# Intermediate stores issued by GpSimd, S5 turns on ScalarE, later direct kernels and an undivided last product in a hybrid S5 and attention block

## The chip, the cores and the metric

The kernel runs on one core of one Trainium2 chip. The metric is device time in microseconds (us) of one launch. The profile comes from one further execution of the same program, recorded by the hardware profiler. The engines are TensorE (PE, matmuls; its weight loads are listed as PEld), VectorE (DVE), ScalarE (ACT), GpSimd (POOL) and SyncE (SP, which here only issues DMAs). Each engine works through its own queue in order; an instruction that waits holds what stands behind it.

## The reference

One layer over 512 tokens of width 2048, in f32:

```python
h = rmsnorm(x, norm_pre[l])
proj = h @ w_in[l]
u_s, g_s, q_d, k_d, v_d, g_d, q_x, g_x = jnp.split(proj, split_at, axis=-1)
y_s = jax.nn.gelu(s5_scan(u_s, ...))               # 64 groups x 16 channels, 64 complex states each
y_s = y_s * jax.nn.sigmoid(y_s @ w_glu[l] + b_glu[l]) * jax.nn.silu(g_s)
y_d = diff_attention(q, k, v, lam, lambda_init, diff_subln[l]) * jax.nn.silu(g_d)   # causal, 4 heads
mem_n = rmsnorm(mem, norm_mem[l])
y_x = memory_attention(q_x, mem_n, w_mem_kv[l]) * jax.nn.silu(g_x)                  # 256 memory tokens
mix = jnp.concatenate([y_s, y_d, y_x], axis=-1) @ w_out[l]
x = x + rmsnorm(mix, norm_post[l])
```

The S5 scan is a linear recurrence with a complex diagonal decay per state, driven through a matrix B, read out through a matrix C, plus a direct term.

## The kernel before, in words

**Weights.** All large matmuls split each f32 operand into a high and a low half and run three passes, high x high, low x high and high x low. A weight chunk is 128 x 1024 f32 (512 KB). SyncE loads it into one of two `raw` buffers, ScalarE casts the high half `whi`, VectorE subtracts to get the low half `wlo` (three buffers each), and TensorE uses both. The matmuls are issued by the helper at line 96, transposes at line 99, and all VectorE, ScalarE and SyncE work by one helper at line 71, so the profile tells instructions apart by their tiles.

**Order.** The list `chunks` holds all weight chunks in order. The main loop goes through it, and each chunk has four units of matmuls. Beside that, `at_slot(n, f)` puts side work into the dictionary `side` behind unit 4n + 3 (n in chunks, fractions being units). A scheduler turns this into the order on each engine; TensorE keeps the program's order of matmuls.

**Stages.** S0 makes the S5 input u, then the memory keys and values (16 chunks of `w_kv`), and prepares the S5 matrices. S5 follows with the gate and query projections (`w_in`) as its chunks and the scan as side work. S1 is the glu of the S5 branch, S2 the rest of `w_in` with the memory attention, S3 the differential attention, S4 the output projection, in which blocks of `w_out` are summed by DMAs from GpSimd (`sum_steps`), and a tail of last products and residual rows.

**S5.** The 64 groups are worked on in eight octets. In S0 each octet gets `s5_products` (line 540: VectorE forms `bp` and, in two halves of the generator, `dp`), `s5_maps` (line 566: four transposes of `bp` and a copy `up`) and `s5_weights` (line 573: small matmuls of `bp` with `dp`, the direct kernels, evacuated to `kz`). `dp`, `up` and `kz` go to DRAM (`sp_dr`, `k_dr`) and come back as `sp` and `tm` when the octet is scanned. In the scan `s5_angles` (line 632) turns the states' angles into cosine and sine in `cs`: the turns `iota` x `ftn`, a reduction by two VectorE instructions, and three activations on ScalarE, ahead of which a table is loaded. `s5_spread` (line 646) copies `up` into four blocks `ub`; `s5_states` (line 652) multiplies them with the input `us` on TensorE, then turns the result with `cs` (tiles `ra`), scans it (`zre`, `zim`) and turns it back into `x`; `s5_outputs` (line 689) multiplies `x` and `tm` out, applies the gelu and stores y in `y_dr`.

**Stores.** Results that a later stage reads again go through DRAM: the u columns, `dp`, `up` and `kz`, the memory keys and values `mk` and `mv`, the projections `ev` (gs, qx and gx), the gated S5 branch `tg` (to `ys_dr`), and the first two column blocks of the output projection (`omx`, to `mix_dr`). All of these are issued by SyncE, in one queue with the loads.

**Tail.** `last_product(i, c0, w)` (line 1267) makes w columns of the last block for token tile i, `c12_evac` and `residual` (line 1247) finish the rows and store them.

Of the kernel before, what the change touches and what calls it, by code (L numbers as in the profile page):

```python
# [19 lines left out]
P = 128  # L20
# [18 lines left out]
LCH = 4  # L39
# [15 lines left out]
def tile_hybrid_block(ctx: ExitStack, tc: tile.TileContext, a: dict, out: bass.AP):  # L55
# [134 lines left out]
    k_dr = [t_.rearrange("p (x e) -> (p x) e", x=4) for t_ in dram("k_dr", 4 * (2 * LCH - 1) * 16, 4)]  # L190
    gs_dr, qx_dr, gx_dr, ys_dr = dram("gs_dr", SEQ, 8), dram("qx_dr", SEQ, 4), dram("gx_dr", SEQ, 4), dram("ys_dr", SEQ, 8)

    chunks, side = [], {}

    def at_slot(n, f):
        side.setdefault(round(4 * n) + 3, []).append(f)
# [84 lines left out]
    def evac_mk():  # L281
        for h in range(4):
            mk = mp.tile([P, NMEM], F32, tag="mk", name="mk", bufs=2)
            v.tensor_tensor(mk, mkacc[h][:, :NMEM], rmb, ALU.mult)
            sy.dma_start(mk_dr[:, h * NMEM:(h + 1) * NMEM], mk)

    def evac_mv(b_, acc):
        mv = mp.tile([P, 512], F32, tag="mv", name="mv", bufs=1)
        s.activation(mv, acc, AF.Copy, scale=rm[:, b_:b_ + 1])
        sy.dma_start(mv_dr[:, b_ * 512:(b_ + 1) * 512], mv)  # L290


    h_raw = {}
# [19 lines left out]
    def evac_u(j, acc):  # L313
        ut = evp["p"].tile([P, LCH, NCH], F32, tag="ev", name="ut", bufs=2)
        v.tensor_tensor(ut, acc.rearrange("p (c s) -> p s c", s=LCH), rbp, ALU.mult)
        sy.dma_start(u_dr[j // 2][(j % 2) * P:(j % 2 + 1) * P], ut.rearrange("p s c -> p (s c)"))

    uacc = {}
    for c in range(NK // 2):
# [35 lines left out]
    def evac_to(dst):  # L355
        def f(i, acc):
            e_ = evp["p"].tile([P, SEQ], F32, tag="ev", name="ev", bufs=2)
            v.tensor_tensor(e_, acc, rb, ALU.mult)
            sy.dma_start(dst, e_)
        return f  # L360

    for j in range(8):
# [177 lines left out]
    def s5_products(o):  # L540


        bc = pt("bc", [512], 2)
        sy.dma_start(bc, a["bc"][o])
        gr = slice(8 * o, 8 * o + 8)

        def powers(t_, n):
            return t_[:, gr, :].unsqueeze(3).to_broadcast([P, 8, n, 16])

        def params(i, n):  # L550
            return bc[:, i * P:(i + 1) * P].rearrange("p (g h) -> p g h", g=8).unsqueeze(2).to_broadcast([P, 8, n, 16])

        bp, dp = pre["bp", o], pre["dp", o] = pt("bp", [8, LCH, 16]), pt("dp", [8, LCH + 1, 16], 2)
        m2 = pt("pm", [8, LCH + 1, 16])
        v.tensor_tensor(bp, powers(w1, LCH), params(0, LCH), ALU.mult)
        v.tensor_tensor(m2[:, :, 0:LCH], powers(w2, LCH), params(1, LCH), ALU.mult)
        v.tensor_tensor(bp, bp, m2[:, :, 0:LCH], ALU.add)
        v.tensor_tensor(dp, powers(pwr, LCH + 1), params(2, LCH + 1), ALU.mult)
        yield
        m2 = pt("pm", [8, LCH + 1, 16])  # L560
        v.tensor_tensor(m2, powers(npwi, LCH + 1), params(3, LCH + 1), ALU.mult)
        v.tensor_tensor(dp, dp, m2, ALU.add)
        sy.dma_start(sp_dr[o][:, 0:640], dp.rearrange("p g j h -> p (g j h)"))
        yield

    def s5_maps(o):
        pp_, up = psum("t"), pt("up", [512])
        for q in range(4):
            transpose(pp_[:, q * P:(q + 1) * P], pre["bp", o][:, 2 * q:2 * q + 2].rearrange("p x b h -> p (x b h)"))
        s.copy(up, pp_)  # L570
        sy.dma_start(sp_dr[o][:, 640:1152], up)

    def s5_weights(o):

        bp, dp, kz = pre["bp", o], pre["dp", o], pre["kz"][o % 2]
        kp = psum("t")
        for x in range(2):
            for q in range(4):
                mm(kp[32 * q:32 * q + 32, x * 64:(x + 1) * 64], bp[:, 2 * q + x, 0:2].rearrange("p b h -> p (b h)"),
                   dp[:, 2 * q + x, 0:LCH].rearrange("p j h -> p (j h)"), start=True, stop=True, tile_position=(0, 32 * q))  # L580
        s.copy(kz[:, :, LCH:], kp[:, 0:P].rearrange("p (x j h) -> p x j h", x=2, h=16)[:, :, 1:])
        for x in range(2):
            v.scalar_tensor_tensor(kz[:, x, LCH - 1], mask16, dsk[:, 2 * o + x:2 * o + x + 1],
                                   kp[:, x * 64:x * 64 + 16], ALU.mult, ALU.add)
        sy.dma_start(k_dr[o // 2].rearrange("(x o p) e -> o p x e", x=2, o=2)[o % 2], kz.rearrange("p x j h -> p x (j h)"))


    def s5_open():
# [43 lines left out]
    def s5_angles(o):  # L632

        cs = t512("cs", 2, (P, 2, 4, P))
        an, kr = cs[:, 0], cs[:, 1]
        g.tensor_tensor(an, iota.unsqueeze(1).to_broadcast([P, 4, P]),
                        ftn[:, 4 * o:4 * o + 4].unsqueeze(2).to_broadcast([P, 4, P]), ALU.mult)
        v.tensor_scalar(kr, an, MAGIC, None, ALU.add)
        v.scalar_tensor_tensor(an, kr, -MAGIC, an, ALU.add, ALU.subtract)
        c_, s_ = (cs[:, i].rearrange("p q c -> p (q c)") for i in range(2))  # L640
        s.activation(s_, c_, AF.Sin, scale=TURN)
        s.activation(c_, c_, AF.Abs)
        s.activation(c_, c_, AF.Sin, scale=-TURN, bias=halfpi)
        oct_[o]["cs"] = (c_, s_)
# [44 lines left out]
    def s5_outputs(o):  # L689

        d, us = s5["d"][o % 2], oct_[o]["us"]
        yp = psum("t")
        cols_ = [slice(q * P, (q + 1) * P) for q in range(4)]
        for q in range(4):
            mm(yp[:, cols_[q]], s5["d"][o // 2 % 2]["tm"][:, 4 * (o % 2) + q], us[:, q], start=q == 0, stop=False,
               skip_group_check=True)
        for q in range(4):
            for x in range(2):
                mm(yp[64 * x:64 * x + 64, cols_[q]], oct_[o]["dp"][:, 2 * q + x, 1:].rearrange("p j h -> p (j h)"),
                   d["x"][:, 2 * q + x, 0:NCH], start=False, stop=True, tile_position=(0, 64 * x), skip_group_check=True)  # L700
        if o % 2 == 0:
            s5["y"] = t512("ysb", 2, (P, 2, 512))
        ysb = s5["y"]
        sq = t512("sq")
        s.activation(sq, yp, AF.Square)
        v.scalar_tensor_tensor(sq, sq, 1.0 / GELU_A, yp, ALU.add, ALU.mult)
        s.activation(sq, sq, AF.Tanh, scale=GELU_A * GELU_S)
        v.scalar_tensor_tensor(ysb[:, o % 2], sq, 1.0, yp, ALU.add, ALU.mult)
        if o % 2 == 1:
            dst = y_dr[o // 2].rearrange("(q x h) (j c) -> j x h q c", x=2, h=16, j=LCH)  # L710
            for x in range(2):
                for j in range(LCH):
# [8 lines left out]
    for o in range(8):  # L721
        e = 9.5 + 1.75 * o if o < 4 else 17.5 + 3.25 * (o - 4)
        d = 2 if o < 4 else 4
        at_slot(e, lambda o=o: (oct_[o].setdefault("pr", s5_products(o)), next(oct_[o]["pr"])))
        at_slot(e + d / 2, lambda o=o: next(oct_[o]["pr"]))
        at_slot(e + 0.75 * d, lambda o=o: s5_maps(o))
        at_slot(e + (2 if o < 4 else 3), lambda o=o: s5_weights(o))
    at_slot(SG - 1, lambda: (s5_open(), s5_load(0), s5_u(0, 0), s5_u(0, 1), s5_load(1)))
    for x in range(2):
        at_slot(SG + 0.5 + x, lambda x=x: s5_toeplitz(0, x))  # L730
# [37 lines left out]
    def evac_glu(j, acc):  # L768
# [9 lines left out]
        v.scalar_tensor_tensor(tg, tg, 1.0, gt, ALU.add, ALU.mult)  # L778
        tgv, tzv = tg.rearrange("p (c t) -> p c t", t=LCH), tz.rearrange("p (t c) -> p c t", t=LCH)
        v.scalar_tensor_tensor(tgv, tzv, 0.125, tgv, ALU.mult, ALU.mult)  # L780
        sy.dma_start(ys_dr[j], tg)

    at_slot(S5_END, ge_open)
    at_slot(S1 + 1.5, rotary_tables)
# [445 lines left out]
    for n, (_, f) in enumerate(chunks):  # L1230
# [155 lines left out]
```

## Time and profile before

| | us |
|---|---|
| median of 3 timed runs | 816.15 (813.62 to 816.22) |
| profiled execution | 812.06 |
| its span | 810.0 |
| TensorE busy | 784.9 (97%) |
| VectorE busy | 590.4 (73%) |
| ScalarE busy | 381.7 (47%) |
| GpSimd busy | 76.5 (9%) |

The granted clock of TensorE is 0.992 on average. The DMA queue that SyncE fills moves 141.39 MB, that of GpSimd 16.78 MB. In the rows of a timeline the first two numbers are the start and the duration in us; a bracket gives the idle time of that engine before the row and what ended it. In the lists of waits the three numbers are the total time, the count and the longest wait. "SPq" and "POOLq" are the DMA-issuing instructions of SyncE and GpSimd.

### The profile page before, as it was taken

Reading aid. Unit: us, or ns where it says so; the run is one execution under the profiler, and the core shown is the slowest. Engines: PE = TensorE matmul, PEld = TensorE weight load, DVE = VectorE, ACT = ScalarE, POOL = GpSimd, SP = SyncE. Lnnn points to the kernel's source line nnn. Section 1 sums busy time; section 2 is a strip of 40 time slices with the busy share of each in tenths; the row PEclk is TensorE's granted clock in tenths of the full one; section 3 lists DMA queues with packets and bytes.
Section 4 is the critical chain, followed back from the end, with each engine's and each line's share of the span. In section 5 each row is a group of like instructions: output and inputs, shape, how many; then the busy total and the mean of one; then the engine's idle time right before and its main releaser. Section 6 shows DMA issues by size and latency. Waiting matters only on the chain.

```text
span 810.0 us, 11040 instructions
## 1 busy us (share of the span) xinstructions
PE 784.9 (97%) x3958; PEld 652.3 (81%) x3958; DVE 590.4 (73%) x1084; ACT 381.7 (47%) x619; POOL 76.5 (9%) x106
## 2 busy tenths in 40 slices
PE   8999999899999999999999999999999999999994
PEld 6877788788878888888877888888888787888884
DVE  4599877748998899846884554657988956774576
ACT  5654433434445445334723543356676643344451
POOL 0000000110000000002111221312201010000001
PEclk9999999999999999999999999999999999999998
DMA  7977767773655565358896854655623515349766
GB/s 250 355 265 259 256 199 248 257 227 89 185 159 158 139 171 160 117 153 299 259 255 239 234 169 144 156 182 159 157 77 103 156 55 205 131 138 330 288 210 254
DMA packets 66486, 158.87 MB, mean 196 GB/s; under 512 B 13568, under 2 KB 27008, under 8 KB 64768
## 3 DMA queue, kind: packets, MB, share of 16 engines
q1 hardware_dynamic: 63616, 141.39, 53.7%
q0 software_dynamic: 2816, 16.78, 8.6%
q8 instruction: 31, 0.51, 0.2%
q14 instruction: 23, 0.19, 0.1%
HBM read 134.68 MB, written 40.24 MB: 216 GB/s over the span
## 4 chain that ended last, share of the span: by engine, by line
PE 73%; DVE 11%; DMA 9%; ACT 3%; issue 2%; SPq 1%; POOL 1%; POOLq 0%; DVEq 0%; ACTq 0%
PE ps_mm L96 60%; PE ps_s L96 6%; PE ps_t L96 6%; DVE wlo L71 3%; DMA raw<-in_w_in_a_dram 2%; ACT whi L71 2%; DMA raw<-in_w_kv_b_dram 2%; DVE sm L71 1%; DMA rows<-in_x_dram 1%; PE ps_t L99 1%; DMA raw<-in_w_kv_a_dram 1%; SPq L71 1%; DVE xr L71 1%; DVE tg L71 1%; DMA raw<-in_w_in_b_dram 1%
## 5 line engine op out<-in xcount | busy, mean ns | idle before, releaser
L71 ACT CAST whi<-raw 128x1024 fp32r<-128x1024 f32 (+1 forms) x135 | 138.8, 1029 | 214.9 <-PE ps_mm L96 109.6
L71 DVE TENSOR_TENSOR wlo<-raw,whi 128x1024 fp32r<-128x1024 f32 (+1 forms) x135 | 161.5, 1198 | 106.9 <-ACT whi L71 106.5
L96 PE MATMUL ps_mm<-hhi,whi 128*128 128x512 f32 x512 | 203.5, 397 | 2.1 <-ACT hhi L71 1.0
L96 PE MATMUL ps_mm<-hlo,whi 128*128 128x512 f32 x512 | 200.7, 392 | 0.8 <-DVE hlo L71 0.8
L96 PE MATMUL ps_mm<-hhi,wlo 128*128 128x512 f32 x512 | 200.9, 392 | 0.0
L96 PEld LDWEIGHTS ps_mm<-hhi,whi 128*128 128x128 f32 x512 | 97.0, 189 | 24.0 <-ACT hhi L71 1.8
L96 PEld LDWEIGHTS ps_mm<-hhi,wlo 128*128 128x128 f32 x512 | 96.7, 189 | 20.9
L96 PEld LDWEIGHTS ps_mm<-hlo,whi 128*128 128x128 f32 x512 | 96.9, 189 | 20.5 <-DVE hlo L71 1.4
L96 PE MATMUL ps_mm<-whi,hhi 128*128 128x512 f32 x128 | 50.3, 393 | 1.1 <-ACT tz L71 0.7
L96 PE MATMUL ps_mm<-wlo,hhi 128*128 128x512 f32 x128 | 50.0, 391 | 0.8 <-DVE wlo L71 0.8
L96 PE MATMUL ps_mm<-whi,hlo 128*128 128x512 f32 x128 | 50.0, 390 | 0.0
L1064 POOL COPY anchor<-whi 128x1 f32<-128x1 f32 x32 | 27.8, 868 | 226.0 <-ACT whi L71 226.0
L96 PEld LDWEIGHTS ps_mm<-whi,hhi 128*128 128x128 f32 x128 | 24.0, 188 | 6.4 <-ACT tz L71 1.2
L96 PEld LDWEIGHTS ps_mm<-wlo,hhi 128*128 128x128 f32 x128 | 24.0, 188 | 5.8 <-DVE wlo L71 1.1
L96 PEld LDWEIGHTS ps_mm<-whi,hlo 128*128 128x128 f32 x128 | 24.0, 188 | 5.1
L71 ACT ACTIVATE pr<-sm,nm 128x128 f32<-128x128 f32 (+3 forms) x32 | 18.0, 564 | 20.8 <-DVE nm L71 20.7
L71 DVE TENSOR_TENSOR x<-ra 64x512 f32<-64x512 f32 x32 | 26.3, 822 | 0.8
L71 DVE TENSOR_TENSOR wlo<-nt,whi 128x1024 fp32r<-128x1024 f32 x12 | 14.7, 1225 | 16.5 <-ACT whi L71 16.5
L96 PE MATMUL ps_mm<-whi,ysh 128*128 128x512 f32 x64 | 25.6, 400 | 0.0
L96 PE MATMUL ps_mm<-gehi,whi 128*128 128x512 f32 x64 | 25.3, 395 | 0.0
L96 PE MATMUL ps_mm<-gehi,wlo 128*128 128x512 f32 x64 | 25.3, 395 | 0.0
L96 PE MATMUL ps_mm<-gelo,whi 128*128 128x512 f32 x64 | 25.3, 395 | 0.0
(348 smaller groups left out, 1530.7 us busy)
## 6 DMA issues: line engine op xcount, KB each, us to landing
raw<-in_w_in_a_dram SPq DMA_DIRECT2D x63, 512.0 KB, 4.3
raw<-in_w_out_b_dram SPq DMA_DIRECT2D x22, 512.0 KB, 3.2
T<-in_w_out_b_dram POOLq DMA_DIRECT2D x16, 512.0 KB, 5.9
raw<-in_w_in_b_dram SPq DMA_DIRECT2D x16, 512.0 KB, 4.2
sp<-sp_dr SPq DMA_DIRECT2D x8, 576.0 KB, 4.8
rows<-in_x_dram SPq DMA_DIRECT2D x4, 1024.0 KB, 7.4
raw<-in_w_kv_a_dram SPq DMA_DIRECT2D x8, 512.0 KB, 3.5
raw<-in_w_kv_b_dram SPq DMA_DIRECT2D x8, 512.0 KB, 4.0
```

The lines of the kernel that those rows point to most:

```text
L71: r = f(*args, **kw)
L96: pin(pe.matmul(*args, **kw))
L99: pin(pe.transpose(o, i, ident))
L1064: m = g.tensor_copy(anchor, now["hi"][:, 0:1])
```

## The change

A helper `store()` issues the stores named above from GpSimd. Given an engine it issues from that engine, three units later than called; only the 32 y stores do so, from SyncE. The turns in `s5_angles` become four ScalarE copies with a scale per row instead of one GpSimd multiply. The maps and weights of an octet move to later slots, for which `bp` gets a second buffer. The last product of the last token tile is one piece of 512 columns instead of two of 256.

```diff
+    chunks, side, pending, now = [], {}, {}, {}
+
+    def store(dst, src, e=None):
+        if e is None:
+            g.dma_start(dst, src)
+        else:
+            pending.setdefault(now["q"] + 3, []).append(lambda: e.dma_start(dst, src))
...
-            sy.dma_start(mk_dr[:, h * NMEM:(h + 1) * NMEM], mk)
+            store(mk_dr[:, h * NMEM:(h + 1) * NMEM], mk)
...
-        bp, dp = pre["bp", o], pre["dp", o] = pt("bp", [8, LCH, 16]), pt("dp", [8, LCH + 1, 16], 2)
+        bp, dp = pre["bp", o], pre["dp", o] = pt("bp", [8, LCH, 16], 2), pt("dp", [8, LCH + 1, 16], 2)
...
-        g.tensor_tensor(an, iota.unsqueeze(1).to_broadcast([P, 4, P]),
-                        ftn[:, 4 * o:4 * o + 4].unsqueeze(2).to_broadcast([P, 4, P]), ALU.mult)
+        for q in range(4):
+            s.activation(an[:, q], iota, AF.Copy, scale=ftn[:, 4 * o + q:4 * o + q + 1])
...
-                    sy.dma_start(dst[j, x], ysb[r0:r0 + 16].rearrange("p o (q c) -> p (o q) c", c=NCH))
+                    store(dst[j, x], ysb[r0:r0 + 16].rearrange("p o (q c) -> p (o q) c", c=NCH), sy)
...
-        at_slot(e + 0.75 * d, lambda o=o: s5_maps(o))
-        at_slot(e + (2 if o < 4 else 3), lambda o=o: s5_weights(o))
+        at_slot(e + (1.75 if o < 4 else 3.75), lambda o=o: s5_maps(o))
+        at_slot(e + (2.75 if o < 4 else 4.25), lambda o=o: s5_weights(o))
...
-            for e in side.get(4 * n + i, []):
+            now["q"] = 4 * n + i
+            for e in pending.pop(now["q"], []) + side.get(now["q"], []):
...
-    acc = last_product(1, 0, 256)
     residual(0, row_scale(0), (1024, 512, 512), (fin["m11"][:, 2], c12[:, 0]))
-    c12_evac(1, acc, 0)
-    acc = last_product(1, 256, 256)
+    acc = last_product(1, 0, 512)
     pre = fin["p"].tile([P, 1], F32, name="pre")
-    v.tensor_reduce(pre, fin["ss"][:, 1, 0:4], AX.X, ALU.add)
+    v.tensor_reduce(pre, fin["ss"][:, 1, 0:3], AX.X, ALU.add)
...
-    v.scalar_tensor_tensor(c12[:, 1, 256:], acc, -1.0, fin["g"][:, 1792:], ALU.mult, ALU.mult)
-    residual(1, sr, (256, 256, 512, 512, 512), (fin["m11"][:, 3], c12[:, 1]))
+    v.scalar_tensor_tensor(c12[:, 1], acc, -1.0, fin["g"][:, 1536:], ALU.mult, ALU.mult)
+    residual(1, sr, (512, 512, 512, 512), (fin["m11"][:, 3], c12[:, 1]))
```

The other stores change as that of `mk` does. How the order on the engines moves, at three places. The first is TensorE in S0 around the weights of octet 0 (`ps_t<-dp,bp`); `whi_792` and `whi_837` (in the change) are weight chunks that follow one another. Before:

```order
L96 MATMUL ps_mm_896<-hhi_82,whi_792 128x512
L96 MATMUL ps_mm_896<-hlo_83,whi_792 128x512
L96 MATMUL ps_mm_896<-hhi_82,wlo_793 128x512
L96 MATMUL ps_t_921<-dp_815,bp_814 32x64 x8
L96 MATMUL ps_mm_896<-hhi_82,whi_792 128x512
```

and in the change:

```order
L96 MATMUL ps_mm_888<-hhi_82,whi_837 128x512
L96 MATMUL ps_mm_888<-hlo_83,whi_837 128x512
L96 MATMUL ps_mm_888<-hhi_82,wlo_838 128x512
L96 MATMUL ps_t_945<-dp_815,bp_814 32x64 x8
L96 MATMUL ps_mm_888<-hhi_82,whi_837 128x512
```

The weights stand 18 rows later, in the next chunk; the transposes of the maps ahead of them (not shown) stand six rows later. On VectorE `dp` keeps its place. The second place is ScalarE in octet 3 of the scan. Before:

```order
L71 CAST whi<-raw 128x1024 [waits DMAHW6_49,PE_49]
L71 COPY ub_1715<-sp 64x4x64 [waits DMAHW5_49]
L71 COPY ub_1715<-sp 64x4x64
L71 ACT_TABLE_LOAD
L71 ACTIVATE cs<-cs 128x512 [waits DVE_49]
L71 COPY ub_1716<-sp 64x4x64
L71 ACTIVATE cs<-cs 128x512 [waits Activation_49]
L71 COPY ub_1716<-sp 64x4x64
L71 ACTIVATE cs<-cs,halfpi 128x512 [waits Activation_49]
```

and in the change (`cs<-cst,ftn` are the turns):

```order
L71 ACTIVATE cs<-cst,ftn 128x128 x4
L71 CAST whi<-raw 128x1024 [waits DMAHW4_49,PE_49]
L71 ACT_TABLE_LOAD [waits DVE_49]
L71 ACTIVATE cs<-cs 128x512 [waits Activation_49]
L71 COPY ub_1702<-sp 64x4x64 [waits DMAHW3_49]
L71 ACTIVATE cs<-cs 128x512 [waits Activation_49]
L71 COPY ub_1702<-sp 64x4x64
L71 ACTIVATE cs<-cs,halfpi 128x512 [waits Activation_49]
L71 COPY ub_1703<-sp 64x4x64 x2
```

The four `ub` copies moved behind the table load and the first `cs`, and the table load now carries the wait for VectorE. Octet 7 has the same order in the change; before, its four copies stood ahead of the table load. In the other octets of the change at least two of the copies, in most all four, stay ahead of it. The third place is GpSimd in S0, whose queue held none of these before:

```order
L197 DMA sp_dr_104<-up 128x512
L197 DMA u_dr_97<-ut 128x512
L197 DMA k_dr_111<-kz_588 128x2x112
L197 DMA sp_dr_105<-dp 128x640
L159 TENSOR_TENSOR rm<-rm,neghalf 128x2
L197 DMA sp_dr_105<-up 128x512
L197 DMA k_dr_111<-kz_590 128x2x112
```

The stores of octets 2 to 4 stand here with the last u store and a GpSimd operation (`rm`) among them. SyncE loses these rows; its weight loads stand in the same order as before, with fewer rows between.

More of the change, by code (lines that the diff above doesn't have):

```diff
@@ L191, in tile_hybrid_block @@
     gs_dr, qx_dr, gx_dr, ys_dr = dram("gs_dr", SEQ, 8), dram("qx_dr", SEQ, 4), dram("gx_dr", SEQ, 4), dram("ys_dr", SEQ, 8)
-    chunks, side = [], {}
+    chunks, side, pending, now = [], {}, {}, {}
[4 more added lines that the diff above has]
+            pending.setdefault(now["q"] + 3, []).append(lambda: e.dma_start(dst, src))
     def at_slot(n, f):
@@ L289, in evac_mv @@
         s.activation(mv, acc, AF.Copy, scale=rm[:, b_:b_ + 1])
-        sy.dma_start(mv_dr[:, b_ * 512:(b_ + 1) * 512], mv)
+        store(mv_dr[:, b_ * 512:(b_ + 1) * 512], mv)
     h_raw = {}
@@ L315, in evac_u @@
         v.tensor_tensor(ut, acc.rearrange("p (c s) -> p s c", s=LCH), rbp, ALU.mult)
-        sy.dma_start(u_dr[j // 2][(j % 2) * P:(j % 2 + 1) * P], ut.rearrange("p s c -> p (s c)"))
+        store(u_dr[j // 2][(j % 2) * P:(j % 2 + 1) * P], ut.rearrange("p s c -> p (s c)"))
     uacc = {}
@@ L358, in f @@
             v.tensor_tensor(e_, acc, rb, ALU.mult)
-            sy.dma_start(dst, e_)
+            store(dst, e_)
         return f
@@ L562, in s5_products @@
         v.tensor_tensor(dp, dp, m2, ALU.add)
-        sy.dma_start(sp_dr[o][:, 0:640], dp.rearrange("p g j h -> p (g j h)"))
+        store(sp_dr[o][:, 0:640], dp.rearrange("p g j h -> p (g j h)"))
         yield
@@ L570, in s5_maps @@
         s.copy(up, pp_)
-        sy.dma_start(sp_dr[o][:, 640:1152], up)
+        store(sp_dr[o][:, 640:1152], up)
     def s5_weights(o):
@@ L584, in s5_weights @@
                                    kp[:, x * 64:x * 64 + 16], ALU.mult, ALU.add)
-        sy.dma_start(k_dr[o // 2].rearrange("(x o p) e -> o p x e", x=2, o=2)[o % 2], kz.rearrange("p x j h -> p x (j h)"))
+        store(k_dr[o // 2].rearrange("(x o p) e -> o p x e", x=2, o=2)[o % 2], kz.rearrange("p x j h -> p x (j h)"))
     def s5_open():
@@ L780, in evac_glu @@
         v.scalar_tensor_tensor(tgv, tzv, 0.125, tgv, ALU.mult, ALU.mult)
-        sy.dma_start(ys_dr[j], tg)
+        store(ys_dr[j], tg)
     at_slot(S5_END, ge_open)
@@ L1074, in sum_steps @@
                 yield
-    now = {}
     anchor = cp.tile([P, 1], F32, name="anchor")
@@ L1096, in out_evac @@
         v.tensor_tensor(mx, acc, fin["g"][:, cs_], ALU.mult)
-        sy.dma_start(mix_dr[tt][:, cs_], mx)
+        store(mix_dr[tt][:, cs_], mx)
     for blk in range(2):
@@ L1285, in tile_hybrid_block @@
     c12_evac(0, acc, 0)
-    acc = last_product(1, 0, 256)
     residual(0, row_scale(0), (1024, 512, 512), (fin["m11"][:, 2], c12[:, 0]))
-    c12_evac(1, acc, 0)
-    acc = last_product(1, 256, 256)
+    acc = last_product(1, 0, 512)
     pre = fin["p"].tile([P, 1], F32, name="pre")
-    v.tensor_reduce(pre, fin["ss"][:, 1, 0:4], AX.X, ALU.add)
+    v.tensor_reduce(pre, fin["ss"][:, 1, 0:3], AX.X, ALU.add)
     v.tensor_scalar(pre, pre, 1.0 / D, EPS, ALU.mult, ALU.add)
-    square(acc, 1, 4)
+    square(acc, 1, 3)
     sr = fin["p"].tile([P, 1], F32, tag="sr", name="sr", bufs=4)
-    v.tensor_scalar(sr, fin["ss"][:, 1, 4:5], 1.0 / D, pre, ALU.mult, ALU.add)
+    v.tensor_scalar(sr, fin["ss"][:, 1, 3:4], 1.0 / D, pre, ALU.mult, ALU.add)
     g.tensor_tensor(sr, sr, neghalf, ALU.pow)
-    v.scalar_tensor_tensor(c12[:, 1, 256:], acc, -1.0, fin["g"][:, 1792:], ALU.mult, ALU.mult)
-    residual(1, sr, (256, 256, 512, 512, 512), (fin["m11"][:, 3], c12[:, 1]))
+    v.scalar_tensor_tensor(c12[:, 1], acc, -1.0, fin["g"][:, 1536:], ALU.mult, ALU.mult)
+    residual(1, sr, (512, 512, 512, 512), (fin["m11"][:, 3], c12[:, 1]))
 def lay_out(inp):
```

## The prediction

> **What bounds the kernel now.** I read the page first, then the waits of TensorE, then the timeline around each wait.
>
> ```profile
> span 810.0 us, 11040 instructions
> PE 784.9 (97%) x3958; PEld 652.3 (81%) x3958; DVE 590.4 (73%) x1084; ACT 381.7 (47%) x619; POOL 76.5 (9%) x106
> PE 73%; DVE 11%; DMA 9%; ACT 3%; issue 2%; SPq 1%; POOL 1%; POOLq 0%; DVEq 0%; ACTq 0%
> ```
>
> TensorE is busy for 97% of the span and is 73% of the chain of waits. The change takes no matmul work away except in the last product, so what it can win is TensorE's idle time, and what it can lose is new idle time. The profiled execution took 812.06 us (810.0 of span and 2.06 around it). The sum below is made against it; the median of the timed runs, 816.15, lies 4.1 higher, and I put the same difference on it. The waits of TensorE that the change touches are these (total, times, longest):
>
> ```profile
> PE ps_t L96 <- DVE dp L71: 3.8, 2, 2.0
> PE ps_s L96 <- ACT ub L71: 1.0, 1, 1.0
> PE ps_t L99 <- DVE bp L71: 0.8, 1, 0.8
> PE ps_t L96 <- DVE rm L71: 0.7, 1, 0.7
> ```
>
> In TensorE's timeline (start, length) they stand here, the last column being the idle time before:
>
> ```profile
> 76.89 0.66 PE L99 MATMUL ps_t<-cst,bp 128*128 128x128 f32 x4 [0.76 <-DVE bp L71]
> 82.29 0.43 PE L96 MATMUL ps_t<-dp,bp 128*32 128x64 f32 x16 [2.00 <-DVE dp L71]
> 111.73 0.43 PE L96 MATMUL ps_t<-dp,bp 128*32 128x64 f32 x16 [0.70 <-DVE rm L71]
> 157.68 0.43 PE L96 MATMUL ps_t<-dp,bp 128*32 128x64 f32 x16 [1.78 <-DVE dp L71]
> ```
>
> All four belong to the S5 direct kernels, the matmuls that the change puts later. Two of them are followed by a clock drop. In the table by stretch (length, then busy time and matmuls of TensorE, further on its granted clock):
>
> ```profile
> 84.00:88.00 4.00, 4.00 (x12) 3.13 (x11) 2.29 (x6) 1.26 (x2) 0.00 (x0) 0.58 1.02 343
> 88.00:110.00 22.00, 22.00 (x148) 18.31 (x148) 19.48 (x32) 9.02 (x17) 0.00 (x0) 1.00 0.56 191
> 159.50:162.50 3.00, 3.00 (x9) 2.32 (x8) 1.22 (x1) 1.28 (x2) 2.64 (x6) 0.51 0.93 279
> ```
>
> At clock 0.58 for 4.0 us and 0.51 for 3.0 us, TensorE loses 4.0 x 0.42 = 1.7 and 3.0 x 0.49 = 1.5 us. The idle times of 2.00 and 1.78 us ended about 2 us before these stretches; the shorter ones have no such stretch behind them.
>
> The Trainium skill ("TensorE: Matmul & The Clock Gate", Part 1) has the array fall to half clock after an idle window of about 3.4 us. The halving agrees with these rows; that 2.0 us of idle time is enough does not, and the rows decide below.
>
> **The change part by part. 1: the direct kernels later (S0, 76 to 163 us).** The order of TensorE shows the maps of octet 0 six matmuls later and its weights 18 later, while VectorE's order around `dp` is the same. 512-wide matmuls start 0.23 us apart (the rows 234.18 and 234.41 in the timeline of octet 3 below), so the maps come 1.4 us later and the weights 4.1 us later than TensorE reaches them now. Both cover the idle times of 0.76 and 2.00 us. The other two fall too, since each weights block moves by at least three units. I add the sequencer's 0.15 us at each of the four (0.92, 2.16, 0.86 and 1.94 in start-to-start terms), 5.9 us, and the two clock drops, 3.2 us: 9.1 us at most. What is late next is the weight load chain, which near the end of this stage is almost as slow as TensorE:
>
> ```profile
> 151.89 1.22 DVE L71 TENSOR_TENSOR wlo<-raw,whi 128x1024 fp32r<-128x1024 f32 x1
> 153.92 0.39 PE L96 MATMUL ps_s<-whi,mhi 128*128 128x512 f32 x1
> ```
>
> The low half of that chunk was ready at 153.11 and used at 153.92, 0.81 us of slack. While the casts wait for TensorE to free a `whi` buffer, the chain moves earlier together with TensorE:
>
> ```profile
> ACT whi L71 <- PE ps_mm L96: 114.4, 50, 4.9
> ```
>
> So most of the gain carries through, and I take off 1.0 us for the chunks behind: **-8.1 us**. The ends are -9.1 and, if the loads don't move at all, 0.81 + 1.94 + 1.5 = 4.2, so -4.2.
>
> **2: the turns on ScalarE (S5, 170 to 345 us).** Each octet loses one GpSimd multiply and gains four ScalarE copies of 128x128. The trace has no such copy; the 64x256 copies of `ub` take 0.40 us and the 128x512 `cs` 0.63, so I take 0.3 each, 1.2 us an octet (0.1 to 0.6 as ends). ScalarE is busy for 47% of the span, 381.7 us, so the 10 us of work find room; 0.6 each would make 19 us and still do. The cost lies in the order behind it. This is octet 3 before, ScalarE, VectorE and TensorE:
>
> ```profile
> 231.71 0.82 ACT L71 COPY ub<-sp 64x256 f32<-64x256 f32 x2
> 232.54 1.28 ACT L71 ACT_TABLE_LOAD   x1
> 234.28 0.63 ACT L71 ACTIVATE cs<-cs 128x512 f32<-128x512 f32 x1 [0.46 <-DVE cs L71]
> 234.82 0.39 ACT L71 COPY ub<-sp 64x256 f32<-64x256 f32 x1
> 235.76 0.40 ACT L71 COPY ub<-sp 64x256 f32<-64x256 f32 x1
> ...
> 233.56 0.68 DVE L71 SCALAR_TENSOR_TENSOR cs<-cs 128x512 f32<-128x512 f32 x1
> ...
> 234.18 0.39 PE L96 MATMUL ps_mm<-hhi,whi 128*128 128x512 f32 x1
> 234.41 0.39 PE L96 MATMUL ps_mm<-hlo,whi 128*128 128x512 f32 x1
> 236.22 1.83 PE L96 MATMUL ps_s<-us,ub 128*128 128x128 f32 x14 [0.96 <-ACT ub L71]
> ```
>
> TensorE's state matmuls wait for the last `ub` copy, which ends at 236.16. Now all four copies stand behind the first `cs`, and the table load ahead of it waits for VectorE's `cs`, which ends at 234.24. Then: table load to 235.55 (1.28), first `cs`, and by the rows (0.54 from `cs` to `ub`, 0.94 from one `ub` to the next with a `cs` between, 0.1 more where that is the longer third one, 0.4 without one) copies at 236.1, 237.05, 238.1 and 238.5, ending at 238.9. That is 2.7 us later, an idle time of 3.8 us, and it is longer than the idle times that brought a clock drop, so 1.6 us (the mean of 1.7 and 1.5) goes with it: +4.3. Octet 7 gets the same order:
>
> ```profile
> 319.57 1.66 ACT L71 COPY ub<-sp 64x256 f32<-64x256 f32 x4
> 321.24 1.28 ACT L71 ACT_TABLE_LOAD   x1
> ...
> 318.95 0.68 DVE L71 TENSOR_TENSOR ra<-zre,cs 128x512 f32<-128x512 f32 x1
> 321.71 0.69 DVE L71 SCALAR_TENSOR_TENSOR cs<-cs 128x512 f32<-128x512 f32 x1
> ...
> 322.72 1.95 PE L96 MATMUL ps_s<-us,ub 128*128 128x128 f32 x16
> ```
>
> Its copies were done at 321.23, 1.5 us early. Now VectorE's `cs` follows the two `ra` directly, at 319.56 to 320.25; table load to 321.53, last copy to 324.9 by the same spacings. TensorE is there at 322.72, so some 2.1 us are lost, with one small matmul between; that is about the length that brought a drop (1.5): +3.6. Together **+7.9 us**; the ends are 0 (copies not late) and +9. In the other octets the copies stay ahead of the table load, and only `cs` comes later, behind which TensorE's next need is microseconds away. VectorE's neighbour on GpSimd is gone, which helps VectorE but no wait of TensorE.
>
> **3: stores through GpSimd, and y stores three units later.** SyncE loses 70 issues and the waits in front of them. The largest kind, and what it does to a load:
>
> ```profile
> SPq L71 <- DVE ev L71: 62.6, 13, 8.8
> ...
> 202.09 0.34 SPq L71 DMA_DIRECT2D gs_dr<-ev  x1
> ...
> 204.93 8.10 SPq L71 DMA_DIRECT2D raw<-in_w_in_a_dram  x3
> ```
>
> The raw load at 204.93 stood behind a store that waited for VectorE. No wait of TensorE in S5 is on a raw load, so here the earlier loads win nothing. They can win in S1, where the casts wait on loads that queue behind the `ys` stores:
>
> ```profile
> 430.56 1.05 ACT L71 CAST whi<-raw 128x1024 fp32r<-128x1024 f32 x1 [1.37 <-DMA raw<-in_w_in_b_dram]
> ```
>
> I take **-1.0 us** of the 1.37 that this cast waited; the ends are 0 and -1.37. Against it stands GpSimd's queue: a `ys` store can now stand behind a transfer of 512 KB that lands late, and ScalarE already waits for those stores:
>
> ```profile
> T<-in_w_out_b_dram POOLq DMA_DIRECT2D x16, 512.0 KB, 5.9
> ACT tg L71 <- DMA ys_dr<-tg: 11.1, 3, 5.7
> ```
>
> Two `tg` buffers at a glu chunk of some 5 us bear 5.9 us of landing, so I charge nothing; up to +2 if they don't.
>
> The Trainium skill ("DMA: Bandwidth & Descriptors", Issuing engines are not separate DMA queues) says that issuing on several engines saves only the sequencer's time to issue. By that alone this part would be 0 and the sum 1.0 higher. The row of 62.6 us shows what the rule leaves out: a store that waits also holds the loads behind it.
>
> **4: the last token tile.** The second half of the last product waits for the first half's evacuation in the same PSUM tile:
>
> ```profile
> 798.79 0.39 PE L96 MATMUL ps_t<-lastyxh,n4h 128*128 128x256 f32 x1 [2.23 <-DVE sr L71]
> 801.96 0.38 ACT L71 ACTIVATE ojk<-ps_t 128x256 f32<-128x256 f32 x1 [4.83 <-PE ps_t L96]
> 805.47 0.74 DVE L71 SCALAR_TENSOR_TENSOR xr<-c,sr,xr 128x512 f32<-128x512 f32 x1
> ```
>
> In one piece TensorE ends some 2.5 us earlier, but VectorE is then held by the residual of the tile ahead until about 802, and its last `xr` ends near 805.3 instead of 806.2: **-0.9 us** (0 to -2.5).
>
> Sum: -8.1 + 7.9 - 1.0 - 0.9 = -2.1, so 809.96 for a profiled execution and 814.0 on the median's scale. About 0.3% (2.4 us) is what a measurement of this kernel can tell from no change.
>
> **The rivals.** *The copies are not late.* The order on ScalarE is fixed, but VectorE's `cs` may come some microseconds earlier against TensorE, as GpSimd's multiply no longer disturbs it. Part 2 is then about 0: -8.1 - 1.0 - 0.9 = -10.0, 806.1. For it speaks that octets 3 and 7 need only 2 to 4 us; against it that VectorE is without a pause from 228 to 236 us in before.
>
> *The loads keep their times (slower).* In S0 SyncE issues a load when VectorE frees the raw buffer, and it does so late in the stage at the pace of the loads. If the chain doesn't follow TensorE forward, part 1 stops at the 0.81 us of slack plus the last stall, -4.2, and the S1 loads win nothing: -4.2 + 7.9 - 0.9 = +2.8, 819.0. It decides from the point where TensorE arrives at a chunk ahead of `wlo`; the row of 114.4 us speaks against it.
>
> *The stalls only move.* VectorE is the engine that is late at 76 to 85 us; if TensorE then waits for it at the next thing instead, part 1 is 0: +6, 822.
>
> *The page's clock rule.* If idle times of 2 us cost no clock, part 1 loses 3.2 and octet 7 its 1.6: -4.9 + 6.3 - 1.0 - 0.9 = -0.5, 815.7. The Trainium skill's page named above gives this; the two stretches at half clock behind such idle times speak against it.
>
> **How the numbers follow.** Forecast 0.42 (814.0, its own range 811.5 to 816.5), copies not late 0.27, loads keep their times 0.20, clock rule 0.07, stalls only move 0.04. Faster by over 0.3% (below 813.7): 0.19 of the forecast and the 0.27, 0.46. Within: 0.19 of the forecast, 0.03 and 0.06 of two rivals, 0.28. Slower: 0.26. The range takes in the first three cases with half a microsecond beyond: 805.5 to 819.5.
>
> **What would show it.** Part 1: no idle time ahead of the `dp,bp` matmuls and clock 1.00 from 80 to 165 us, with S5 starting some 8 us earlier. Part 2: TensorE idle for 3 to 4 us ahead of `us,ub` in octet 3 and about 2 in octet 7, each with a clock near 0.5 behind it. Part 3: no `ev` on SyncE's list of waits. Part 4: one block of 512-wide matmuls without the idle 2.23. I am wrong if the `ub` waits stay near 1 us, or if S0 ends less than 5 us earlier.

## The result, and the profile after

The changed kernel takes 826.3 us (median of 6 runs, 821.58 to 827.25), the kernel before 814.14 us (6 runs); the ratio is 1.0139 with a 95% interval of 1.0111 to 1.0166. It is slower, by some 12 us. The profiled execution has a span of 824.5 us against 810.0.

The page of the changed kernel, its span, busy times and chain of waits:

```profile
span 824.5 us, 11060 instructions
PE 789.4 (96%) x3934; PEld 655.0 (79%) x3934; DVE 588.6 (71%) x1082; ACT 389.6 (47%) x649; POOL 108.9 (13%) x168
PE 66%; DVE 16%; DMA 8%; ACT 5%; issue 3%; POOL 1%; SPq 0%; DVEq 0%; POOLq 0%; ACTq 0%
```

TensorE's share of the chain fell from 73% to 66%, VectorE's rose from 11% to 16%. The waits of TensorE (total, times, longest):

```profile
PE ps_s L96 <- ACT ub L71: 6.3, 4, 3.1
PE ps_mm L96 <- DVE wlo L71: 5.2, 1, 5.2
PE ps_s L96 <- DVE wlo L71: 3.1, 1, 3.1
PE ps_mm L96 <- ACT tz L71: 2.2, 1, 2.2
```

The waits on `bp`, `dp` and `rm` that stood here before are gone. New are `wlo` with 5.2 us at once, and `ub` and `wlo` ahead of the state matmuls (`ps_s<-us,ub`). State matmuls read `us` and `ub`; the 3.1 us that the list puts down to `wlo` stand in octet 7 and end 0.05 us behind a `ub` copy too (below). Where the time went is seen from TensorE's arrival at fixed points of the program in both traces:

| TensorE (unless said) at | before | changed | difference |
|---|---|---|---|
| first matmul of the memory keys | 105.52 | 108.25 | +2.7 |
| last matmul but one of the memory values | 159.10 | 158.26 | -0.8 |
| states of octet 0 | 174.74 | 174.84 | +0.1 |
| states of octet 4 | 257.74 | 262.89 | +5.2 |
| first glu matmul | 368.25 | 379.60 | +11.4 |
| first matmul of the tail product | 788.08 | 800.85 | +12.8 |
| end of VectorE's last `xr` | 806.21 | 818.05 | +11.8 |
| last store landed | 809.05 | 821.11 | +12.1 |
| end of the span | 809.96 | 824.48 | +14.5 |

So S0 gains nothing, S5 loses 11.3 us, S1 to S4 lose 1.4, the tail gains 0.9, and behind the last landed store 2.5 us are added. Traces also differ ahead of everything that was changed: VectorE's first `ut` starts at 52.95 us before, at 52.45 in the changed kernel and between 51.42 (run 3) and 54.40 (run 7) in the experiments. A lead of 1 to 2 us at one point therefore shows nothing by itself; where it matters, times from the first `ut` are given beside it.

**The loss in S0.** The chain of waits between 50 and 76 us in the changed kernel:

```profile
52.53 1.92 DVE ut L71 x2
...
54.77 8.60 DMA u_dr<-ut
...
63.46 1.06 DVE ut L71
...
69.15 1.15 DVE wlo L71
70.29 0.04 issue
70.34 5.91 PE ps_mm L96 x13
```

A u store issued at 54.77 takes 8.60 us to land, and the one ahead of it 7.7. There are two `ut` buffers, so VectorE can't evacuate the next columns of u, and its queue with the angle work and `wlo` behind it is late. SyncE's issues at the same place, before and then changed, show what else was on the way:

```profile
54.02 1.29 SPq L71 DMA_DIRECT2D u_dr<-ut  x2
...
61.53 0.55 SPq L71 DMA_DIRECT2D mT<-in_memT_dram  x1
62.13 0.46 SPq L71 DMA_DIRECT2D bc<-in_bc_dram  x1
62.63 0.43 SPq L71 DMA_DIRECT2D rows<-in_mem_dram  x1
65.38 5.02 SPq L71 DMA_DIRECT2D raw<-in_w_in_a_dram  x2
```

```profile
53.28 0.42 SPq L71 DMA_DIRECT2D mT<-in_memT_dram  x1
53.75 0.44 SPq L71 DMA_DIRECT2D bc<-in_bc_dram  x1
54.23 0.63 SPq L71 DMA_DIRECT2D rows<-in_mem_dram  x1
70.31 0.33 SPq L71 DMA_DIRECT2D raw<-in_w_in_a_dram  x1
```

Before, the loads of `mT`, `bc` and `rows` stood behind u stores that waited for VectorE, and went out at 61.5 to 62.6. With the stores gone from SyncE they went out at 53.3 to 54.2, at the moment of the u stores (53.8 and 54.8). The third and fourth u store, issued by GpSimd too but at 62.99 and 64.81, when all of these loads but `rows` had landed, took 2.8 and 2.3 us. TensorE's 5.2 us of idle time was followed by a stretch at clock 0.63:

```profile
72.00:78.00 6.00, 6.00 (x18) 4.69 (x18) 5.89 (x17) 2.95 (x3) 0.00 (x0) 0.63 0.36 132
```

The slow stretch begins with the first matmul behind the idle time: from 70.34 to 76.47 the 512-wide matmuls start 0.44 us apart, against 0.23 us otherwise, which is 3.0 us lost in 14 of them.

**The loss in S5** is at octets 3 and 7, where the prediction put it. Octet 3, the timelines of ScalarE, VectorE and TensorE in the changed kernel:

```profile
235.04 1.28 ACT L71 ACT_TABLE_LOAD   x1 [3.08 <-DVE cs L71]
236.34 0.63 ACT L71 ACTIVATE cs<-cs 128x512 f32<-128x512 f32 x1
236.87 0.39 ACT L71 COPY ub<-sp 64x256 f32<-64x256 f32 x1
...
238.87 0.81 ACT L71 COPY ub<-sp 64x256 f32<-64x256 f32 x2
...
234.28 0.68 DVE L71 SCALAR_TENSOR_TENSOR cs<-cs 128x512 f32<-128x512 f32 x1
...
238.27 0.49 PE L96 MATMUL ps_s<-us,ub 128*128 128x128 f32 x2 [3.09 <-ACT ub L71]
239.74 1.57 PE L96 MATMUL ps_s<-us,ub 128*128 128x128 f32 x8 [0.98 <-ACT ub L71]
```

The table load waits 3.08 us for VectorE's `cs`, and all four `ub` copies wait behind it. A stretch at half clock follows (240.00 to 243.00, below).

```profile
240.00:243.00 3.00, 3.00 (x16) 2.90 (x16) 0.75 (x2) 0.00 (x0) 0.00 (x0) 0.55 0.40 147
```

Octet 7 has the same picture:

```profile
327.93 1.28 ACT L71 ACT_TABLE_LOAD   x1 [3.12 <-DVE cs L71]
...
331.15 0.49 PE L96 MATMUL ps_s<-us,ub 128*128 128x128 f32 x2 [3.13 <-DVE wlo L71]
```

Its second `ub` copy ends at 331.10, and a second idle time of 0.97 us follows.

### The profile page after: what moved, and what is told of

It is laid out like the page before. It is cut to its first block, busy times and chain, and to the rows that moved or that the text cites. A ratio compares the mean times of both kernels' runs of the same rounds, so it can differ in the third digit from the quotient of the medians.

```text
span 824.5 us, 11060 instructions
## 1 busy us (share of the span) xinstructions
PE 789.4 (96%) x3934; PEld 655.0 (79%) x3934; DVE 588.6 (71%) x1082; ACT 389.6 (47%) x649; POOL 108.9 (13%) x168
## 4 chain that ended last, share of the span: by engine, by line
PE 66%; DVE 16%; DMA 8%; ACT 5%; issue 3%; POOL 1%; SPq 0%; DVEq 0%; POOLq 0%; ACTq 0%
PE ps_mm L96 52%; PE ps_s L96 8%; PE ps_t L96 5%; DVE wlo L71 3%; DVE ra L71 2%; DMA raw<-in_w_in_a_dram 2%; DVE sm L71 2%; PE ps_t L99 1%; DMA rows<-in_x_dram 1%; ACT whi L71 1%; DMA us<-u_dr 1%; ACT cs L71 1%; DMA u_dr<-ut 1%; DVE x L71 1%; DVE xr L71 1%
## 5 line engine op out<-in xcount | busy, mean ns | idle before, releaser
L1070 POOL COPY anchor<-whi 128x1 f32<-128x1 f32 x32 | 30.2, 943 | 134.6 <-ACT whi L71 134.5
L71 DVE TENSOR_TENSOR ra<-ps_s,cs 128x512 f32<-128x512 f32 x32 | 20.9, 685 | 13.2 <-PE ps_s L96 4.6
L96 PE MATMUL ps_s<-us,ub 128*128 128x128 f32 x128 | 18.9, 306 | 9.4 <-ACT ub L71 6.3
L96 PEld LDWEIGHTS ps_s<-us,ub 128*128 128x128 f32 x128 | 17.8, 216 | 11.5 <-ACT ub L71 9.4
```

Of the source, the lines that this page charges most:

```text
L71: r = f(*args, **kw)
L96: pin(pe.matmul(*args, **kw))
L1070: m = g.tensor_copy(anchor, now["hi"][:, 0:1])
```

## The experiments

After the result I held that three separate losses add: late u stores (some 8 us), `ub` behind the table load (11.3 us), and GpSimd's queue at the end and in S1. The rival was that GpSimd's stores disturb everything a little. Where the 9 us that the later direct kernels should give had gone was a question of its own. Each ratio below is against the kernel before on the same chip. The changed kernel was not timed again beside the runs; its distance from a run is given by the medians, which are of different times, and by the two ratios (1.0139 for the changed kernel).

**1. u stores back on SyncE** (in the changed kernel).

```diff
-        store(u_dr[j // 2][(j % 2) * P:(j % 2 + 1) * P], ut.rearrange("p s c -> p (s c)"))
+        sy.dma_start(u_dr[j // 2][(j % 2) * P:(j % 2 + 1) * P], ut.rearrange("p s c -> p (s c)"))
```

> The changed kernel with only the eight u stores issued by SyncE again. Theory A (late u stores: with their waits gone from SyncE the loads behind them start first, the u stores then take 7.7 and 8.6 us to land where they took 3.0 and 2.6, the two ut buffers stay full, VectorE idles 4.7 us and its late weight halves cost TensorE 5.3 us and a clock drop): the TensorE idle time at 70 us is gone and the time falls by 6 to 8 us against the changed kernel. Theory B (the software queue disturbs the whole stage, all its stores together): it falls by less than 3 us and the idle time stays or moves.

816.4 us, ratio 1.0083 (1.0051 to 1.0116): about 10 us less than the changed kernel by the medians, 4.6 by the ratios, so the size of the gain is open on either side of the 6 to 8 us expected. The idle time at 70 us is gone and TensorE is at the memory keys at 99.25, 6.3 us ahead of before; from the first `ut` it is there 8.3 us sooner than in the changed kernel. The first two u stores land in 2.3 and 2.2 us. At octet 0 the lead on before is 7.4 us (6.2 from the first `ut`); octets 3 and 7 then take it away.

**2. `ub` copies ahead of the turns** (in the changed kernel).

```diff
-        at_slot(e - 0.5, lambda o=o: s5_spread(o))
+        at_slot(e - 1, lambda o=o: s5_spread(o))
```

> The changed kernel with the ub copies put into the slot ahead of the turns (two units earlier), so that they stand ahead of the turns, of the table load and of cs in every octet. Theory A (what costs is that the copies stand behind the table load that waits for VectorE): the idle times of TensorE ahead of the state matmuls in octets 3 and 7 (4.4 us each with their clock drops 1.7 us each) are gone, 10 to 12 us less than the changed kernel. Theory B (ScalarE's added work or the later cs is what costs): the wait stays with VectorE's cs or moves to the output matmuls, less than 4 us gained.

812.7 us, ratio 1.0016 (0.9994 to 1.0039), some 14 us less than the changed kernel by the medians and 10 by the ratios. The waits ahead of the states of octets 3 and 7 are gone. The u loss is still there, and octet 0 now waits 3.3 us for its `us` load:

```profile
PE ps_mm L96 <- DVE wlo L71: 5.8, 2, 5.6
PE ps_s L96 <- DMA us<-u_dr: 3.3, 1, 3.3
```

**3. The later direct kernels alone** (in the kernel before).

```diff
-        bp, dp = pre["bp", o], pre["dp", o] = pt("bp", [8, LCH, 16]), pt("dp", [8, LCH + 1, 16], 2)
+        bp, dp = pre["bp", o], pre["dp", o] = pt("bp", [8, LCH, 16], 2), pt("dp", [8, LCH + 1, 16], 2)
...
-        at_slot(e + 0.75 * d, lambda o=o: s5_maps(o))
-        at_slot(e + (2 if o < 4 else 3), lambda o=o: s5_weights(o))
+        at_slot(e + (1.75 if o < 4 else 3.75), lambda o=o: s5_maps(o))
+        at_slot(e + (2.75 if o < 4 else 4.25), lambda o=o: s5_weights(o))
```

> The kernel before with only the later slots of maps and weights and the second bp buffer. Theory A (the prediction's part 1): the four waits of TensorE on bp, dp and rm between 76 and 158 us and both clock drops are gone, 7 to 9 us less than before. Theory B (the loads keep their times): the gain stops at about 4 us. Theory C (the stalls only move to another wait on VectorE): within 2 us of before.

813.2 us, ratio 1.0004 (0.9978 to 1.0029): no difference. TensorE leads by 7.2 us at the same matmul of the memory values and by 1.4 at the states of octet 0; from the first `ut` that is 5.7 us and nothing. A wait for `diag` of 2.1 us (1.1 before) with a stretch at clock 0.72 behind it (112 to 118) takes part of the lead, octet 0 the rest:

```profile
PE ps_s L96 <- ACT cs L71: 6.1, 1, 6.1
...
163.69 0.33 SPq L71 DMA_DIRECT2D raw<-in_w_in_a_dram  x1
164.11 0.38 SPq L71 DMA_DIRECT2D sp<-sp_dr  x1
164.54 6.75 SPq L71 DMA_DIRECT2D us<-u_dr  x8
```

The list names `cs`, which ended on ScalarE at 173.16, but that stood behind a `ub` copy that had waited for the `sp` load (landed at 170.98), and the last `us` load landed at 173.06; TensorE starts at 173.30. Both loads are octet 0's. SyncE issued its `sp` load at 164.11, in the kernel before at 163.83:

```profile
163.39 0.38 SPq L71 DMA_DIRECT2D raw<-in_w_in_a_dram  x1
163.83 0.45 SPq L71 DMA_DIRECT2D sp<-sp_dr  x1
```

Seven microseconds of lead on TensorE moved it by nothing, because it stands behind weight loads, and the last three of these went out as VectorE ended a `wlo` (156.26, 159.32 and 163.65). There is one more of them than before: in run 3, and in run 7 below, the scheduler put 41 weight loads ahead of octet 0's `sp` load, in all other kernels here 40. The last one waited until 163.69, where the entry ahead of it had gone out at 160.24; some 3 us of the delay stand at it. A half-clock stretch follows (0.50 from 172 to 178), and at the first glu matmul run 3 is 1.0 us behind before.

**4. The stores alone** (in the kernel before: `store()` and all that call it, as in the diff of the change).

```diff
-            sy.dma_start(mk_dr[:, h * NMEM:(h + 1) * NMEM], mk)
+            store(mk_dr[:, h * NMEM:(h + 1) * NMEM], mk)
```

> The kernel before with only the stores moved (to GpSimd, and the y stores three units later). Theory A (late u stores, late ys stores, a longer end): TensorE idles some 5 us near 70 us with a clock drop behind it, and 2 us in the glu stage, and the end behind the last landed store is 2.4 us longer: 8 to 11 us more than before. Theory B (the stores are harmless without the other parts): within 3 us of before.

819.9 us, ratio 1.0111 (1.0080 to 1.0141): 7 us more than before by the medians, a little under what I expected, and 9 by the ratio, within it. The wait of 5.2 us on `wlo` is there, the end behind the last landed store is 3.65 us where it was 0.91, and octet 0's states come 3.2 us later than before.

**5. Both repairs** (1 and 2 together, the two diffs above).

> The changed kernel with both repairs: u stores on SyncE and ub copies ahead of the turns. Theory A (the three losses are separate and add): the 7.4 us that the kernel with u on SyncE led before by at octet 0 stay to the end, without the 11 us of octets 3 and 7; less 0.9 in the tail, plus 1.7 at the end behind the last landed store: 804 to 807, 6 to 8 us less than before. Theory B (what is won early is taken back by the loads further on): within 2.4 us of before.

804.5 us, ratio 0.9908 (0.9881 to 0.9935): faster than both kernels, and inside the range that the adding of the three losses gave. Octet 0's states come at 166.46, 8.3 us ahead of before, and the lead is 9.4 us at the first glu matmul (358.80). SyncE, changed kernel with both repairs:

```profile
155.66 0.33 SPq L71 DMA_DIRECT2D raw<-in_w_in_a_dram  x1
156.10 0.37 SPq L71 DMA_DIRECT2D sp<-sp_dr  x1
156.52 6.40 SPq L71 DMA_DIRECT2D us<-u_dr  x8
```

The `sp` load goes out at 156.10, 7.7 us ahead of before.

**6. Both repairs, turns on GpSimd again.**

```diff
-        for q in range(4):
-            s.activation(an[:, q], iota, AF.Copy, scale=ftn[:, 4 * o + q:4 * o + q + 1])
+        g.tensor_tensor(an, iota.unsqueeze(1).to_broadcast([P, 4, P]),
+                        ftn[:, 4 * o:4 * o + 4].unsqueeze(2).to_broadcast([P, 4, P]), ALU.mult)
```

> As the kernel with both repairs, but the turns computed by GpSimd again. Theory A (with the copies ahead the place of the turns is off the path): within 2 us of the kernel with both repairs. Theory B (the turns on ScalarE relieve VectorE, whose reductions ran 0.7 us longer beside GpSimd, or start octet 0 earlier): 3 us or more slower than it.

805.7 us, ratio 0.9915 (0.9885 to 0.9944), not to be told from run 5. With the copies ahead it doesn't matter which engine computes the turns. The turns on ScalarE alone, in the kernel before, were not run.

**7. Both repairs, all stores on SyncE, y stores at once.** Every store is changed like these two:

```diff
-        store(sp_dr[o][:, 640:1152], up)
+        sy.dma_start(sp_dr[o][:, 640:1152], up)
...
-                    store(dst[j, x], ysb[r0:r0 + 16].rearrange("p o (q c) -> p (o q) c", c=NCH), sy)
+                    sy.dma_start(dst[j, x], ysb[r0:r0 + 16].rearrange("p o (q c) -> p (o q) c", c=NCH))
```

> As the kernel with both repairs, but all stores on SyncE again and the y stores at once. Theory A (moving the other stores off SyncE is what lets octet 0's sp and us loads go out some 6 us earlier): TensorE waits about 6 us for octet 0 as in the later slots alone, against which the end behind the last store is 1.7 us shorter: 3 to 5 us slower than the kernel with both repairs. Theory B (the stores don't matter once octet 0 is set up by the later slots): it is 1 to 2 us faster than it.

809.6 us, ratio 0.9961 (0.9931 to 0.9991), 5 us more than run 5. Octet 0 waits again, and its states come at 174.91, as before:

```profile
PE ps_s L96 <- DMA us<-u_dr: 4.7, 1, 4.7
```

So in these runs the later kernels win in S0 only where the stores have left SyncE as well and octet 0's loads go out earlier. How much of that is the stores themselves is not shown: run 7 also has the 41st weight load ahead of `sp` (issued at 166.00, the entry ahead of it at 162.95), and `diag` with the clock behind it costs it some 2 us that run 5 doesn't lose. The y stores, three units later in the change, were put back here with the others and never run alone.

**8. u stores issued by ScalarE** (in the changed kernel), a hardware queue apart from SyncE's (the page lists it with 2.10 MB of its own).

```diff
-        store(u_dr[j // 2][(j % 2) * P:(j % 2 + 1) * P], ut.rearrange("p s c -> p (s c)"))
+        s.dma_start(u_dr[j // 2][(j % 2) * P:(j % 2 + 1) * P], ut.rearrange("p s c -> p (s c)"))
```

> The changed kernel with the u stores issued by ScalarE, a hardware queue of its own. Theory A (crowding: the loads that no longer stand behind the stores fill the DMA engines): the stores still take 6 us or more to land, TensorE still idles 3 us or more near 70 us, and the time stays above 821. Theory B (GpSimd's software queue itself is slow): they land in about 3 to 4 us, the idle time is gone and the time is near that with u on SyncE, 816.

822.6 us, ratio 1.0128 (1.0065 to 1.0192), above 821, as the first theory has it. The first two u stores take 6.7 and 6.9 us to land (7.7 and 8.6 from GpSimd, 3.0 and 2.6 before, 2.3 and 2.2 in run 1), VectorE waits and TensorE idles 3.4 us:

```profile
59.80 1.05 DVE L71 TENSOR_TENSOR ut<-ps_mm,rb 128x512 f32<-128x512 f32 x1 [3.14 <-DMA u_dr<-ut]
```

Most of the lateness therefore comes with the loads that run at the same time, from whichever queue the stores are issued. This is what the Trainium skill ("DMA: Bandwidth & Descriptors", Issuing engines are not separate DMA queues) says of DMAs of different engines: they run on the same DMA engines and interleave. The 6.7 us agree with it. The other 1.0 and 1.7 us can be GpSimd's queue or the `rows` load, which goes out at 59.72 here and at 54.23 in the changed kernel; the runs don't tell these apart.

**9. Both repairs and the ys stores on SyncE.**

```diff
-        store(ys_dr[j], tg)
+        sy.dma_start(ys_dr[j], tg)
```

> The kernel with both repairs, with the eight ys stores on SyncE too (86 DMAs issued by GpSimd, 94 with both repairs, 102 in the changed kernel, 32 before). Theory A (a ys store on GpSimd's queue lands behind a 512 KB transfer and so ScalarE's tg and then tz are late): the wait of TensorE on tz in the glu stage, 1.5 us with both repairs, falls to about 0.9 as before; the end behind the last landed store gets some 0.3 us shorter: about 1 us faster than with both repairs. Theory B (the waits on tz come from elsewhere): no difference.

803.2 us, ratio 0.9887 (0.9858 to 0.9915), the lowest of all, though its interval overlaps that of run 5 and it was timed on another chip. The wait on `tz` did not fall: 1.6 us with the ys stores on SyncE, 1.3 in run 5. Runs 1 and 6, with the ys stores on GpSimd, have none and 0.3 us. What this wait hangs on in S1 stays open. The end behind the last landed store fell from 2.67 to 1.79 us.

**10. Both repairs, only S0's stores on GpSimd** (u, ev, ys and mix on SyncE; beside run 9's line:)

```diff
-            store(dst, e_)
+            sy.dma_start(dst, e_)
...
-        store(mix_dr[tt][:, cs_], mx)
+        sy.dma_start(mix_dr[tt][:, cs_], mx)
```

> The kernel with both repairs, with only the stores of dp, up, kz, mk and mv left on GpSimd (62 DMAs issued by it), the u, ev, ys and mix stores on SyncE. Theory A (what counts for octet 0 are the stores of S0, and the end grows with the count of GpSimd's DMAs, 0.03 us of waiting for GpSimd with 32, 1.3 with 94, 1.65 with 102): octet 0 as early as with both repairs, the wait for GpSimd at the end 0.6 us or less: 1 to 2 us faster than with both repairs. Theory B (the end doesn't depend on the count): the end stays at 2.6 us behind the last landed store.

804.8 us, ratio 0.9918 (0.9890 to 0.9946). Octet 0 keeps most of its lead (167.72, 7.0 us ahead of before), the end falls to 1.35 us, but S1 has two waits on `tz`, 3.4 us together. The expected 1 to 2 us are not there.

**11. Three buffers for `ut` and `ev`** (in the changed kernel), timed once.

```diff
-        ut = evp["p"].tile([P, LCH, NCH], F32, tag="ev", name="ut", bufs=2)
+        ut = evp["p"].tile([P, LCH, NCH], F32, tag="ev", name="ut", bufs=3)
...
-            e_ = evp["p"].tile([P, SEQ], F32, tag="ev", name="ev", bufs=2)
+            e_ = evp["p"].tile([P, SEQ], F32, tag="ev", name="ev", bufs=3)
```

> The changed kernel with three instead of two buffers for ut and ev. Theory A (VectorE waits at the third u evacuation for the buffer of the first): it now waits at the fourth, for the same store, so it has some 1.9 us more work done by then, and TensorE's idle time at 70 us falls from 5.3 to between 3 and 4 us. Theory B (VectorE is slowed by GpSimd there, not by the buffer): 5.3 us as in the changed kernel.

824.5 us, with 4.9 us of idle time at 70 us, not 3 to 4. VectorE does wait one evacuation later, at the fourth, and for the first store, as it must if the buffer holds it:

```profile
62.24 1.06 DVE L71 TENSOR_TENSOR ut<-ps_mm,rb 128x512 f32<-128x512 f32 x1 [5.69 <-DMA u_dr<-ut]
```

But the store lands at 62.15 anyway, so the fourth starts 1.2 us earlier than in the changed kernel and the angle work and `wlo` behind it only 0.4 us. The place of the wait agrees with the theory, the gain was worked out wrongly.

## Why the prediction was wrong

The forecast was 814.0 on the median of before, -2.1 us; measured were +12.

**Part 1, "-8.1 us" for the later kernels.** The four waits and both clock drops are gone, and run 3 has a lead of 7.2 us at the end of S0 (5.7 from the first `ut`, behind a new loss at `diag`), so the working up to there held. The step that failed is "What is late next is the weight load chain ... I take off 1.0 us for the chunks behind". Late next were octet 0's `sp` and `us` loads, which SyncE issues behind the last weight loads of S0. I read the slack of a chunk's `wlo` and never that of the first state matmuls. In run 3 TensorE waits 6.1 us there and the gain ends at nothing. The rival "the loads keep their times" had the mechanism at the end of S0, with another victim and too small a price. In the change itself the stores leave SyncE too, and with the u stores out of the way 8.3 us do arrive at octet 0 (run 5). That the -8.1 is met there is luck: the working had nothing that moves octet 0's loads.

**Part 3, "-1.0 us" for the stores.** This is the step that turned the sign. I counted what leaves SyncE's queue and looked at `ys` in S1 for what could be late on GpSimd's, and missed the other side: the loads that had stood behind the u stores run ahead and compete with them. I had charged "nothing" for late stores, with +2 as the end. The u stores cost TensorE 5.2 us of idle time and 3.0 us of clock, 8.2 together, and run 1 gives 8.3 back. S1 to S4 are 1.4 us worse where I had -1.0; the wait on `tz` there is 2.2 us, against 0.7 before, with a clock of 0.57 behind it (431 to 435). That the stores cause this is not shown, since runs 1, 2 and 6 have the same stores there and spend 0.7 to 1.8 us less than before between the same two points. And the end of the program is 2.5 us longer, a place that I hadn't read at all. What the move of the stores goes with, octet 0's loads some 6 us earlier (157.53 in run 1, 163.83 before), I had not seen either. In the changed kernel it is covered by the loss at 70 us.

**Part 2, "+7.9 us" for the turns.** Mechanism, place and order of the `ub` copies were right: predicted was their end at 238.9 in octet 3, 2.7 us late; measured are 3.25 us more of idle time and 1.75 of clock, 5.0 us instead of 4.3. Octet 7 costs 6.2 instead of 3.6: I took VectorE's `cs` from its time before, but VectorE had by then become 2.5 us later against TensorE, and the lost time is 4.4 us (idle times of 3.13 and 0.97 and the sequencer's part) instead of 2.1. Measured together +11.3. The rival "the copies are not late" is out; run 2 shows it from the other side.

**Part 4, "-0.9 us" for the tail.** Measured -0.9, with VectorE as the bound, as said.

The sum with what was measured: +0.1 for S0 with the handover, +11.3, +1.4, -0.9, and 2.7 from the last `xr` on: +14.5 in the span. Told from the forecast: -2.1, then +8.2 for the u stores, +3.4 for octets 3 and 7, +2.4 for S1 to S4 and +2.7 at the end make +14.6.

The prediction weighed what the Trainium skill ("TensorE: Matmul & The Clock Gate", Part 1) states, half clock after an idle window of about 3.4 us, against rows with idle times of 1.8 and 2.0 us. In the runs here all idle times of 3 us and more in the stream of matmuls were followed by a drop. Run 1 has one of 1.8 us (its wait for octet 0's `us` load) with the clock at 1.00 from 165 to 180 us, while run 3's 2.1 us at `diag` brought one. So idle times of about 2 us bring a drop in some places and not in others, and taking one for granted was too sure.

## What to carry to other kernels

An instruction that waits in a load queue is also a brake: take it out and the loads behind it start earlier, into whatever else is on the DMA engines then. So look for what these loads will collide with, and for the buffers that wait for it. When a stall is removed, follow the lead to the next place where several things must have arrived (here the first matmuls of the next stage), not only along the chain that was next before. And when work is added to an engine, read the order of everything behind it: here four small copies of 1.3 us an octet put other copies behind a table load that waits, and two octets lost 11 us by it.

## What the runs showed that I had not expected

The end of the program grows with the DMAs that GpSimd issues. From the last landed store to the end of the span it takes 0.91 to 0.97 us with 32 of them (before, runs 3 and 7), 1.35 with 62, 1.79 with 86, 2.60 to 2.69 with 94 and 3.37 to 3.65 with 102. In the changed kernel SyncE is done at 822.1 and GpSimd's next instruction comes at 823.7. What fills the time is a `DRAIN`, which GpSimd's sequencer starts with its last work. Before and then changed, the numbers behind the count being the shortest, the median and the longest in ns:

```profile
L1382 POOLq DRAIN  x3: 40/102/3276, 802.7 to 809.7; - x3
L1386 POOLq DRAIN  x3: 51/93/9000, 814.7 to 824.2; - x3
```

The long one takes 3.28 us with 32 DMAs, 5.73 with 62, 7.70 with 86, 8.34 or 8.35 with 94 (four kernels) and 9.00 with 102 (four kernels), so 0.08 us more for each DMA, whichever stores they are. Before, it ended at 806.00, ahead of the last landing store (809.05), and cost nothing. In the changed kernel it ends at 823.69, 2.6 us behind that store. With 62 it ends 0.7 us ahead of the last store, with 86 it ends 1.0 us behind.
